# The down projection of a SwiGLU block: five contraction groups, the last by plain products, in place of four groups of Strassen products

## The chip, the cores and the metric

The kernel runs on one core of one Trainium2 chip. The metric is the device time of one execution in microseconds; 3 runs of the kernel before have a median of 3491.99 us (3489.88 to 3497.54). TensorE is called PE here, VectorE DVE, ScalarE ACT, GpSimd POOL and SyncE SP; SP issues nearly all DMAs.

## The reference, cut to what matters

One layer of a hybrid backbone for 640 tokens (512 of a latent grid, 128 of context): adaLN, attention beside a recurrent mixer, output projection, post-norm, and then the SwiGLU block, with D_MODEL = 2048 and D_FF = 5632. The change lies in the last lines of it:

```python
def _swiglu(h, p):
    return (jax.nn.silu(h @ p["w_ffn_gate"]) * (h @ p["w_ffn_up"])) @ p["w_ffn_down"]

    x = _post_norm(x, g1, _merge(att, rw, p), p["ln1_g"], p["ln1_b"])
    x = _post_norm(x, g2, _swiglu(x * (1 + sc2) + sh2, p), p["ln2_g"], p["ln2_b"])
```

`_post_norm` is a layer norm of ALPHA * x + gate * f over the 2048 features.

## The kernel before, in words

Everything is kept transposed, features on the 128 partitions and the 640 tokens along the free axis, in two halves of 320 columns (`H1`, `H2`, also called half 0 and half 1). Every fp32 matrix product is made of three fp32r matmuls, high by high, high by low and low by high, so each operand is split into a rounded part (ACT, a cast, line 1302 for the weights) and a rest (DVE, a subtraction, line 227).

The three products of the SwiGLU block go by Strassen's scheme in Winograd's form: two row tiles of the output by two column halves are made from seven products of sums of quarters instead of eight. `strassen` (from line 1451) makes one such block. It takes its weights from `Quads`, whose generator `units` loads the four quarters of a weight block (`raw`, 10 buffers), forms the three sums on POOL and DVE, splits each of the seven (`qh`, `ql`, 4 buffers each) and yields them one by one, three ahead of PE. `ORDER` (1, 7, 5, 6, 4, 2, 3) is the order of the seven products. A product of n pairs of contraction tiles is 3n matmuls of 128x128 weights by 320 columns into one PSUM bank (`b`, 8 banks).

The contraction of the down projection has 44 tiles, 22 pairs. While the gate and up projections run, `stored` writes each pair of hidden tiles to DRAM (`h_d`) as seven tiles of 128x640: splits of the quarters and of their sums. Afterwards the down projection goes in groups, `sizes = ((4, 1), (6, 2), (6, 2), (6, 2))`: pairs in the group and weight granules a round. A group is 8 rounds, j = 0 to 7, each for two row tiles of the output, so a round is 7 x 3 x 4 = 84 or 7 x 3 x 6 = 126 matmuls. The output (`z`, two tiles of 128x640 a round) starts from the normed input, and is loaded from DRAM one round ahead, added to by DVE (`gated`), and, in all groups but the last, stored to DRAM one round later (`sums_ahead`, `sums_behind`, driven by `moved` between products).

The operands of a group (tile `op`, 128x640 fp32, 7 for a pair) live in a pool of `N_F` = 63 slots that the `z` tiles share. `Fetch` loads them for the next group while one runs: one load at every second weight unit, up to `room` = 63 - 7 * pairs - 7, set in round 1 (round 3 of the first group), and in round 7 one at every unit as slots are given back. What is not loaded by then is loaded by `operand` when a product first asks for it. SP's order is the program's in this stage, so such a load stands behind what the program issued earlier, among it the store of the round before.

The last group is made in two passes, so that one half can be finished early. The first pass makes products 1, 7, 5, 6 and 3 for all rounds (90 matmuls each; half 1 is then complete and its sums for the layer norm, `norms[1].add`, go on DVE, ACT and POOL). The second pass, `rest`, makes products 2 and 4 (36 matmuls a round) in an order of PE that is fixed by hand; between its rounds PE also makes the sums of half 1 (after j = 1) and spreads mean and deviation (after j = 2), and then 16 tiles of half 1 are finished: on POOL an addition of the mean, on DVE a multiplication, on ACT scale and bias, a store. At the end half 0 is finished in the same way.

Of the kernel before, what the change touches and what calls it, by code (L numbers as in the profile page):

```python
# [8 lines left out]
F32 = mybir.dt.float32  # L9
# [6 lines left out]
P = 128  # L16
# [74 lines left out]
DONE1 = 0  # L91
NORM2 = "GTGV"
# [66 lines left out]
def step_kernel(ctx: ExitStack, tc: tile.TileContext, a: dict, o: dict, upto: int = 99, npairs: int = NPAIR, dbg=None):  # L159
# [1183 lines left out]
    class Quads:  # L1343


        def __init__(self, gen):
            self.gen = gen(self)
            self.buf, self.beside = [], None
            for _ in range(N_Q - 1):
                self.push()  # L1350
# [24 lines left out]
        def plain(self, srcs):  # L1375
            raw = []
# [7 lines left out]
        def units(self, pairs, begun=0, later=0):  # L1384


            nxt = None
            for n, src in enumerate(pairs):
                ng = src.shape[1]
                gs = range(ng)  # L1390
                whole = n < len(pairs) - later
# [27 lines left out]
                for g in gs:  # L1419
                    if whole:  # L1420
                        yield self.split(q[3, g])
                    del q[3, g]
                ahead(3)
                for g in gs:
                    if n >= begun and whole:
# [25 lines left out]
    def strassen(qs, ops, ng, out, u1=None, whole=True, beside=None):  # L1451

# [3 lines left out]
        for m in [m for m in ORDER if (m > 2 or u1 is None) and (whole or m not in (2, 4))]:  # L1456
# [4 lines left out]
            elif m == 6:  # L1461
# [5 lines left out]
                if not whole:  # L1467
                    out(0, 0, None, u1)
                    out(1, 0, None, u3)
# [104 lines left out]
    z_d = [[dram.tile([P, NT], F32, name=f"zd{c}{j}") for j in range(16)] for c in range(4)]  # L1574
# [3 lines left out]
    w_pairs += [a["w_down4"][j] for j in range(8)]  # L1578
    w_pairs += [a["w_down"][j][:, 2 * c: 2 * c + 2] for c in range(3) for j in range(8)]

    def sequence(q):
# [16 lines left out]
        yield from q.units(w_pairs, N_PRE, 8)  # L1598
        yield from q.plain(w[k, g] for w in w_pairs[-8:] for k in (1, 3) for g in range(2))
# [113 lines left out]
    def stored(i, b1, b2):  # L1713

        def put(n, x, hi, lo):
# [3 lines left out]

        p1 = fslot("p1", F32R)  # L1720
# [15 lines left out]
    class Fetch:  # L1736
# [3 lines left out]
        def __init__(self, k0, n):  # L1740
            self.k0, self.t, self.room, self.count = k0, [[None] * 7 for _ in range(n)], 0, 0
            self.every, self.turn = 2, 0
            self.order = [(i, m) for q in ((0,), (1, 2), (3, 4), (5, 6)) for i in range(n) for m in q]
# [15 lines left out]
        def operand(self, i, m):  # L1759
# [4 lines left out]
            return (t[0][:, H1], t[0][:, H2]) if q == 0 else (t[q][:, hs], t[q + 1][:, hs])  # L1764

# [52 lines left out]
    sizes = ((4, 1), (6, 2), (6, 2), (6, 2))  # L1818
# [14 lines left out]
    def moved(c, j, n):  # L1833

        rel = fetch.released(n) if fetch and j == 7 else None
        for k in range(len(ORDER)):
            if k == 4:
                sums_behind()
            if k == 3 and (c, j) != (3, 7):
# [8 lines left out]
    for c, (npr, ng) in enumerate(sizes):  # L1848
        ops, k0 = fetch, k0 + npr
        fetch = qs.beside = Fetch(k0, sizes[c + 1][0]) if c < 3 else None  # L1850
# [173 lines left out]
```

## Time and profile before

| | us |
|---|---|
| median of 3 runs (range) | 3491.99 (3489.88 to 3497.54) |
| the profiled execution | 3500.31 |
| its span, first to last instruction | 3498.5 |
| PE busy in the span | 3255.5 |
| first and last matmul of the down projection | 2857.4 and 3469.7 |

The profile is that of one execution, with times from the span's start. "Busy" is the time in which at least one instruction of the engine runs; matmuls overlap, so a mean of 309 ns for one says how long it takes, not how often one starts. A view by stages gives busy time and count (x) of each engine in a stretch, the share of its clock that TensorE was granted, the mean busy share of the 16 DMA engines and the rate. In a view of groups, "| 43.8, 647 | 7.0" is busy time in us, mean ns of one, and idle time ahead of them. A view of waits gives the total, the times and the longest.

### The profile page before, as it was taken

Reading aid. Unit: us, or ns where it says so; the run is one execution under the profiler, and the core shown is the slowest. Engines: PE = TensorE matmul, PEld = TensorE weight load, DVE = VectorE, ACT = ScalarE, POOL = GpSimd, SP = SyncE. Lnnn points to the kernel's source line nnn. Section 1 sums busy time; section 2 is a strip of 40 time slices with the busy share of each in tenths; the row PEclk is TensorE's granted clock in tenths of the full one; section 3 lists DMA queues with packets and bytes.
Section 4 is the critical chain, followed back from the end, with each engine's and each line's share of the span. In section 5 each row is a group of like instructions: output and inputs, shape, how many; then the busy total and the mean of one; then the engine's idle time right before and its main releaser. Section 6 shows DMA issues by size and latency. Waiting matters only on the chain. (4 is left out here: it accounts for less than half of the span.)

```text
span 3498.5 us, 71287 instructions
## 1 busy us (share of the span) xinstructions
PE 3255.5 (93%) x27538; PEld 2961.4 (85%) x27538; DVE 2555.3 (73%) x4562; ACT 1480.9 (42%) x3115; POOL 1070.4 (31%) x1106
## 2 busy tenths in 40 slices
PE   7988998999999689999979999999999999999987
PEld 4677676777877578899979999999999999999886
DVE  1356766776766676468688888888888888778798
ACT  1144443443443454455454444444444444334334
POOL 0021222122122132102164444444444442212245
PEclk9998999999999899999999999999999999999997
DMA  8754444444211211085434443444443478776743
GB/s 300 240 175 137 142 147 139 161 160 139 66 61 59 72 34 36 31 270 179 142 116 144 155 136 127 134 132 138 133 128 125 144 252 293 255 250 207 256 128 108
DMA packets 289717, 529.06 MB, mean 151 GB/s; under 512 B 31008, under 2 KB 83680, under 8 KB 289376
## 3 DMA queue, kind: packets, MB, share of 16 engines
q1 hardware_dynamic: 289376, 524.49, 45.3%
q8 instruction: 216, 3.54, 0.4%
q14 instruction: 125, 1.02, 0.1%
HBM read 429.65 MB, written 93.09 MB: 149 GB/s over the span
## 5 line engine op out<-in xcount | busy, mean ns | idle before, releaser
L227 DVE TENSOR_TENSOR ql<-raw,qh 128x512 fp32r<-128x512 f32 (+1 forms) x1136 | 930.6, 833 | 263.6 <-ACT qh L1302 242.5
L1302 ACT CAST qh<-raw 128x512 fp32r<-128x512 f32 (+1 forms) x1136 | 660.2, 588 | 913.2 <-PE b L113 777.8
L227 POOL TENSOR_TENSOR raw<-raw,raw 128x512 f32<-128x512 f32 (+1 forms) x288 | 394.4, 1371 | 849.6 <-DVE ql L227 662.2
L113 PE MATMUL b<-t,qh 128*128 128x320 f32 x2816 | 621.7, 310 | 8.6 <-ACT qh L1302 7.3
L113 PE MATMUL b<-op,qh 128*128 128x320 f32 x2464 | 545.9, 315 | 18.2 <-DMA op<-hd 18.0
L113 PEld LDWEIGHTS b<-t,qh 128*128 128x128 f32 x2816 | 471.5, 188 | 10.1 <-ACT qh L1302 8.1
L113 PE MATMUL b<-p,qh 128*128 128x320 f32 x2112 | 468.2, 310 | 0.0
L113 PE MATMUL b<-t,ql 128*128 128x320 f32 x1408 | 435.3, 310 | 6.4 <-DVE ql L227 6.2
L113 PEld LDWEIGHTS b<-op,qh 128*128 128x128 f32 x2464 | 417.9, 192 | 24.6 <-issue 12.3
L113 PE MATMUL b<-op,ql 128*128 128x320 f32 x1232 | 375.3, 316 | 20.1 <-DVE ql L227 20.0
L113 PEld LDWEIGHTS b<-p,qh 128*128 128x128 f32 x2112 | 355.2, 189 | 0.2 <-ACT qh L1302 0.2
L113 PE MATMUL b<-p,ql 128*128 128x320 f32 x1056 | 328.5, 311 | 8.5 <-DVE ql L227 8.5
L113 PEld LDWEIGHTS b<-t,ql 128*128 128x128 f32 x1408 | 264.4, 188 | 8.8 <-DVE ql L227 8.8
L113 PEld LDWEIGHTS b<-op,ql 128*128 128x128 f32 x1232 | 232.4, 191 | 28.5 <-DVE ql L227 28.0
L113 PE MATMUL b<-mh,qh 128*128 128x320 f32 x1024 | 231.0, 315 | 6.4 <-ACT qh L1302 6.2
L113 PE MATMUL acc<-xh,whi 128*128 128x320 f32 x928 | 233.3, 334 | 3.3 <-ACT P L1165 2.5
L113 PE MATMUL acc<-xl,whi 128*128 128x320 f32 x928 | 235.5, 336 | 0.0
L113 PE MATMUL acc<-xh,wlo 128*128 128x320 f32 x928 | 234.3, 335 | 0.0
L227 DVE TENSOR_TENSOR raw<-raw,raw 128x512 f32<-128x512 f32 (+1 forms) x288 | 217.6, 768 | 12.7 <-POOL raw L227 10.8
L113 PEld LDWEIGHTS b<-p,ql 128*128 128x128 f32 x1056 | 199.3, 189 | 11.2 <-DVE ql L227 11.2
L264 ACT CAST whi<-raw 128x512 fp32r<-128x512 f32 (+1 forms) x156 | 94.9, 608 | 232.8 <-PE acc L113 143.8
L113 PEld LDWEIGHTS b<-mh,qh 128*128 128x128 f32 x1024 | 175.4, 192 | 7.6 <-ACT qh L1302 6.8
(331 smaller groups left out, 5686.1 us busy)
## 6 DMA issues: line engine op xcount, KB each, us to landing
wm<-in_w_mod_dram SPq DMA_DIRECT2D x64, 1024.0 KB, 5.3
op<-hd SPq DMA_DIRECT2D x154, 320.0 KB, 5.7
raw<-in_w_gate_dram SPq DMA_DIRECT2D x188, 256.0 KB, 2.7
raw<-in_w_up_dram SPq DMA_DIRECT2D x188, 256.0 KB, 2.9
raw<-in_w_down_dram SPq DMA_DIRECT2D x224, 192.0 KB, 2.8
raw<-in_w_in_dram SPq DMA_DIRECT2D x132, 256.0 KB, 2.7
wm<-in_w_mod_dram SPq DMA_DIRECT2D x64, 512.0 KB, 6.2
raw<-in_w_out_dram SPq DMA_DIRECT2D x128, 256.0 KB, 3.0
```

The source lines that it names most:

```text
L113: self.eng.matmul(out, lhsT, rhs, start=start, stop=stop)
L227: eng.tensor_tensor(out=out, in0=x, in1=y, op=op)
L264: A.copy(hi, r)
L1302: A.copy(hi, x)
```

## The change

The groups become 4, 4, 4, 4 and 6 pairs. The first four go by Strassen as before, with one weight granule of 128x512 a round (the weights of 16 pairs are laid out so, not of 4). The last, six pairs, goes by eight plain products: `stored` writes four tiles for each of its pairs, not seven, and `Fetch` loads four. For rounds 0 to 3 `plain` makes both halves at once, in two banks from the same weights (144 matmuls a round); for rounds 4 to 7 half 1 alone (72), and then, in the order fixed by hand, half 0 of rounds 4 to 7, whose weights are loaded and split a second time. The sums of half 1 stand after j = 4 of that last pass, its spread and finish after j = 5. There is a fifth set of `z` tiles in DRAM.

```diff
+LAST = 6
-        def units(self, pairs, begun=0, later=0):
+        def units(self, pairs, begun, follow):
...
+                    elif follow:
+                        self.first.append(self.load(follow.pop(0)))
...
-    def strassen(qs, ops, ng, out, u1=None, whole=True, beside=None):
+    def strassen(qs, ops, ng, out, u1=None, beside=None):
...
-    def rest(qs, ops, ng, out):
-        for m, n in ((0, 2), (1, 4)):
-            out(m, 0, product(qs, ops, ng, n), None)
+    def plain(qs, ops, ng, halves, out):
+
+        npr = len(ops) // ng
+        for m in range(2):
+            ps = [bank()[:, :HN] for _ in halves]
+            for q in range(2):
+                for g in range(ng):
+                    wh, wl = qs.get()
+                    for k in range(npr):
+                        cs_ = slice(k * P, k * P + P)
+                        for t, n in zip(ps, halves):
+                            xh, xl_ = ops.plain(g * npr + k, q, n)
+                            for i, (w, x) in enumerate(((wh, xh), (wh, xl_), (wl, xh))):
+                                T.matmul(t, w[:, cs_], x, start=q + g + k + i == 0,
+                                         stop=q == 1 and i == 2 and k == npr - 1 and g == ng - 1)
+            for t, n in zip(ps, halves):
+                out(m, n, t, None)
...
-    w_pairs += [a["w_down4"][j] for j in range(8)]
-    w_pairs += [a["w_down"][j][:, 2 * c: 2 * c + 2] for c in range(3) for j in range(8)]
+    w_pairs += [a["w_down4"][j][:, c: c + 1] for c in range(4) for j in range(8)]
+    w_pairs += [a["w_down"][j] for j in range(8)]
...
-        yield from q.units(w_pairs, N_PRE, 8)
-        yield from q.plain(w[k, g] for w in w_pairs[-8:] for k in (1, 3) for g in range(2))
+
+        last = [w[k, g] for w in w_pairs[-8:] + w_pairs[-4:] for k in range(4) for g in range(2)]
+        yield from q.units(w_pairs[:-8], N_PRE, last)
+        yield from q.plain(last)
...
+        if i >= NF2 - LAST:
+            put(0, b1, fslot("p1", F32R), fslot("p1", F32R))
+            yield
+            put(2, b2, fslot("p2", F32R), fslot("p2", F32R))
+            return
...
-    sizes = ((4, 1), (6, 2), (6, 2), (6, 2))
+    sizes = (4, 1), (4, 1), (4, 1), (4, 1), (6, 2)
...
+    for j in range(8):
+        if j == 1:
+            loads.close()
+        z = ahead.pop((4, j))
+        if j == 0:
+            sums_behind()
+        if j < 7:
+            sums_ahead(4, j + 1)
+        plain(qs, ops, ng, (1, 0) if j < 4 else (1,), gated(5, 2 * j, z))
+        z1 += z
+        del z
+        summed(1, j)
+        if j < 4:
+            summed(0, j)
...
+    for j in range(4, 8):
+        plain(qs, ops, ng, (0,), gated(5, 2 * j, z1[2 * j: 2 * j + 2]))
+        for z in z1[2 * j: 2 * j + 2]:
+            norms[0].add(z)
+        if j == 4:
+            sums = norms[1].sums()
+        elif j == 5:
+            norms[1].spread(norms[1].stats(*sums, LN_EPS / ALPHA ** 2))
+            for f in range(KT):
+                finish(f, 1)
```

Up to the last pairs of the hidden layer the instructions stand on each engine as before. Three places show what moves.

SP before, in the first round of the third group (`hd105` is tile 5 of pair 10, the first pair of that group; `raw` are weights, `zd` the store of the round before):

```order
L1366 DMA raw_6806_36810<-in_w_down_dram 128x384
L1831 DMA zd214_17281<-z_6676_36272 128x640
L1831 DMA zd215_17282<-z_6677_36274 128x640
L1752 DMA op_6813_36835<-hd105_17156 128x640
L1752 DMA op_6814_36837<-hd106_17157 128x640
L1752 DMA op_6815_36842<-hd115_17163 128x640
L1752 DMA op_6816_36844<-hd116_17164 128x640
L1752 DMA op_6817_36849<-hd125_17170 128x640
L1752 DMA op_6818_36851<-hd126_17171 128x640
L1366 DMA raw_6819_36856<-in_w_down_dram 128x384
```

SP after, at the same stores, in the first round of the third group of four pairs (8 to 11; `hd116` is its last operand, `hd120` the first of the next group):

```order
L1770 DMA op_6574_35843<-hd115_17163 128x640
L1770 DMA op_6579_35866<-hd116_17164 128x640
L1367 DMA raw_6586_35905<-in_w_down4_dram 128x512
L1367 DMA raw_6590_35924<-in_w_down4_dram 128x512
L1367 DMA raw_6594_35944<-in_w_down4_dram 128x512
L1614 DMA z_6600_35971<-zd22_17269 128x640
L1614 DMA z_6601_35973<-zd23_17270 128x640
L1367 DMA raw_6603_35976<-in_w_down4_dram 128x512
L1855 DMA zd214_17281<-z_6522_35637 128x640
L1855 DMA zd215_17282<-z_6523_35639 128x640
L1770 DMA op_6619_36049<-hd120_17165 128x640
```

Before, 16 of the 42 operands of this group are issued only in its first round (six of them here), 18 in that of the second group and 16 in that of the fourth; after, 7 of the 28 operands of the second group, and none of the third, the fourth and the last.

PE before, in the last group's first pass, one product in one bank (`op_7271` and `op_7272` are high and low part of an operand):

```order
L113 MATMUL b_7555_39968<-op_7271_38795,qh_7545_39928 128x320
L113 MATMUL b_7555_39968<-op_7272_38797,qh_7545_39928 128x320
L113 MATMUL b_7555_39968<-op_7271_38795,ql_7546_39929 128x320
L113 MATMUL b_7555_39968<-op_7273_38802,qh_7545_39928 128x320
L113 MATMUL b_7555_39968<-op_7274_38804,qh_7545_39928 128x320
L113 MATMUL b_7555_39968<-op_7273_38802,ql_7546_39929 128x320
```

PE after, in the last group's rounds of both halves:

```order
L114 MATMUL b_7197_38541<-op_7081_38041,qh_7192_38515 128x320
L114 MATMUL b_7197_38541<-op_7091_38083,qh_7192_38515 128x320
L114 MATMUL b_7197_38541<-op_7081_38041,ql_7193_38516 128x320
L114 MATMUL b_7198_38542<-op_7081_38041,qh_7192_38515 128x320
L114 MATMUL b_7198_38542<-op_7091_38083,qh_7192_38515 128x320
L114 MATMUL b_7198_38542<-op_7081_38041,ql_7193_38516 128x320
```

One split of the weights (`qh`, `ql`) now serves six matmuls a tile, in two banks, where it served three.

DVE before, where the finish of half 1 begins (`ns` from `b` is the mean; `z` by `ns` the finish, `nd` and `ns` the sums of half 0, `ql` a weight's rest):

```order
L227 TENSOR_TENSOR ns_5956_33218<-b_40495,nc_33217 128x320
L227 TENSOR_TENSOR ns_5957_33219<-ns_5957_33219,nq_40481 128x320
L227 TENSOR_TENSOR z_38546<-z_38546,ns_5957_33219 128x320
L227 TENSOR_TENSOR ql_40592<-raw_40426,qh_40591 128x384
L227 TENSOR_TENSOR z_38548<-z_38548,ns_5957_33219 128x320
L236 SCALAR_TENSOR_TENSOR z_39234<-b_40573,mod,z_39234 128x320
L227 TENSOR_TENSOR z_38820<-z_38820,ns_5957_33219 128x320
L227 TENSOR_TENSOR ql_40609<-raw_40443,qh_40608 128x384
```

DVE after, at the same place:

```order
L228 TENSOR_TENSOR ns_5941_33164<-b_40315,nc_33163 128x320
L228 TENSOR_TENSOR ns_5942_33165<-ns_5942_33165,nq_40301 128x320
L228 TENSOR_TENSOR z_38460<-z_38460,ns_5942_33165 128x320
L228 TENSOR_TENSOR ql_40412<-raw_40248,qh_40411 128x384
L228 TENSOR_TENSOR z_38462<-z_38462,ns_5942_33165 128x320
L228 TENSOR_TENSOR z_38537<-z_38537,ns_5942_33165 128x320
L228 TENSOR_TENSOR ql_40427<-raw_40263,qh_40426 128x384
L228 TENSOR_TENSOR z_38539<-z_38539,ns_5942_33165 128x320
```

From this `ns` to the last `ns` of half 0 stand 64 instructions before (16 `z` by `ns`, 16 `ql`) and 42 after (16 and 12); 180 matmuls of the projection are still to come on PE before, 144 after.

More of the change, by code (lines that the diff above doesn't have):

```diff
@@ L1347, in __init__ @@
             self.gen = gen(self)
-            self.buf, self.beside = [], None
+            self.buf, self.beside, self.first = [], None, []
             for _ in range(N_Q - 1):
@@ L1375, in plain @@
         def plain(self, srcs):
-            raw = []
+            raw, self.first = self.first, []
             for src in srcs:
@@ L1449, in begin @@
         out(0, 0, product(qs, ops, ng, 2), u1)
-    def strassen(qs, ops, ng, out, u1=None, whole=True, beside=None):
+    def strassen(qs, ops, ng, out, u1=None, beside=None):
         bk = {}
-        for m in [m for m in ORDER if (m > 2 or u1 is None) and (whole or m not in (2, 4))]:
+        for m in [m for m in ORDER if m > 2 or u1 is None]:
             ps = bk[m] = product(qs, ops, ng, m)
@@ L1573, in step_kernel @@
     h_d = [[dram.tile([P, NT], F32, name=f"hd{j}{n}") for n in range(7)] for j in range(NF2)]
-    z_d = [[dram.tile([P, NT], F32, name=f"zd{c}{j}") for j in range(16)] for c in range(4)]
+    z_d = [[dram.tile([P, NT], F32, name=f"zd{c}{j}") for j in range(16)] for c in range(5)]
     w_pairs = []
@@ L1742, in __init__ @@
             self.every, self.turn = 2, 0
-            self.order = [(i, m) for q in ((0,), (1, 2), (3, 4), (5, 6)) for i in range(n) for m in q]
+            kinds = ((0, 1), (2, 3)) if k0 == NF2 - LAST else ((0,), (1, 2), (3, 4), (5, 6))
+            self.order = [(i, m) for q in kinds for i in range(n) for m in q]
         def __len__(self):
@@ L1859, in step_kernel @@
             for _ in beside:
                 pass
-            if c < 3:
-                behind += [(c, 2 * j + m, z[m]) for m in range(2)]
-            else:
-                z1 += z
+            behind += [(c, 2 * j + m, z[m]) for m in range(2)]
             del z
-            if c == 3 and j:
-                for z in z1[2 * j: 2 * j + 2] if j > 1 else z1[:4]:
-                    norms[1].add(z)
-        if c == 3:
-            order = ExitStack()
-            order.enter_context(tc.manual_schedule(engines={mybir.EngineType.PE}))
-            for j in range(8):
-                rest(qs, ops, ng, gated(5, 2 * j, z1[2 * j: 2 * j + 2]))
-                if j:
-                    for z in z1[2 * j: 2 * j + 2] if j > 1 else z1[:4]:
-                        norms[0].add(z)
-                if j == 1:
-                    sums = norms[1].sums()
-                elif j == 2:
-                    norms[1].spread(norms[1].stats(*sums, LN_EPS / ALPHA ** 2))
-                    for f in range(KT):
-                        finish(f, 1)
-            order.close()
@@ L1884, in step_kernel, with summed @@
-        del ops
+        del ops
+    def summed(n, j):
+        if j:
+            for z in z1[2 * j - 2 * (j == 1): 2 * j + 2]:
+                norms[n].add(z)
+    for j in range(8):
[12 more added lines that the diff above has]
+            summed(0, j)
@@ new lines, in step_kernel @@
+    order = ExitStack()
+    order.enter_context(tc.manual_schedule(engines={mybir.EngineType.PE}))
+    for j in range(4, 8):
[8 more added lines that the diff above has]
+                finish(f, 1)
+    order.close()
```

32 lines of the change are left out of this document (16 added, 16 removed).

## The prediction

> **What bounds the kernel now.** The page comes first.
>
> ```profile
> span 3498.5 us, 71287 instructions
> PE 3255.5 (93%) x27538; PEld 2961.4 (85%) x27538; DVE 2555.3 (73%) x4562; ACT 1480.9 (42%) x3115; POOL 1070.4 (31%) x1106
> ```
>
> PE is busy for 93% of the span, so time lies in its work or in its few waits. The profiled execution took 3500.31 us around this span; the median of the runs is 3491.99, 0.2% less. Next the view of one tile, `op`, which every matmul of the down projection reads.
>
> ```profile
> L113 PE MATMUL b<-op,qh x2464: 302/309/636, 2857.4 to 3469.6; 128*128 128x320 f32 x190
> L113 PE MATMUL b<-op,ql x1232: 303/309/637, 2857.7 to 3469.7; 128*128 128x320 f32 x176
> ```
>
> All 3696 are there (22 pairs x 7 products x 8 rounds x 3), so counting them off in order dates every round (rounds are counted from 0). The view of stages below is cut at such rounds. A row starts with the stretch and its length, then PE, PEld, DVE, ACT and POOL busy, the clock, the DMA share and GB/s.
>
> ```profile
> 2700.00:2800.00 100.00, 100.00 (x684) 100.00 (x683) 82.82 (x112) 43.88 (x77) 44.03 (x33) 1.00 0.41 132
> 2857.38:2908.82 51.44, 50.41 (x338) 49.32 (x337) 46.00 (x86) 26.26 (x44) 15.96 (x12) 1.00 0.89 323
> 2908.82:2958.11 49.29, 49.29 (x339) 49.29 (x337) 43.97 (x87) 21.93 (x38) 13.18 (x9) 1.00 0.83 293
> 2958.11:2988.50 30.39, 23.62 (x129) 20.25 (x128) 17.73 (x39) 7.22 (x15) 4.17 (x4) 0.89 0.86 315
> 2988.50:3117.86 129.36, 129.36 (x885) 129.36 (x884) 107.19 (x214) 52.52 (x105) 31.14 (x28) 1.00 0.65 219
> 3117.86:3145.16 27.30, 21.93 (x129) 20.41 (x128) 16.85 (x35) 7.31 (x15) 3.97 (x4) 0.87 0.91 326
> 3274.51:3298.45 23.94, 17.79 (x92) 16.02 (x91) 16.99 (x32) 5.47 (x11) 7.76 (x6) 0.79 0.88 310
> 3298.45:3409.48 111.03, 99.29 (x633) 94.21 (x633) 101.44 (x191) 43.30 (x92) 47.64 (x37) 0.98 0.48 156
> 3414.76:3430.05 15.29, 15.09 (x116) 14.30 (x115) 15.29 (x33) 7.11 (x16) 8.68 (x7) 1.00 0.43 121
> 3430.05:3469.71 39.66, 32.44 (x180) 30.59 (x180) 38.69 (x62) 21.33 (x43) 27.40 (x25) 0.83 0.34 111
> 3469.71:3498.50 28.79, 17.96 (x59) 10.58 (x57) 19.69 (x33) 11.10 (x20) 12.90 (x13) 0.55 0.26 92
> ```
>
> The second group's rounds 1 to 7 are 882 matmuls in 129.36 us: 146.7 ns each, PE without a gap. Rounds 4 to 7 of the first group (336 in 49.29) keep the same pace. Against it the other stretches lose: start of group one 51.44 - 49.28 = 2.2; first round of groups two, three and four 11.9, 8.8 and 10.7 (126, 126 and 90 matmuls); the rest of group four's first pass, 630 matmuls, 18.6; rounds 1-2 of its second pass, 72 matmuls, 4.7; rounds 3-7, 180 matmuls, 13.3. That is 70 us of stall. The view of waits, from 2840 us on, names the two causes:
>
> ```profile
> PE b L113 <- DVE ql L227: 20.0, 25, 1.7
> PE b L113 <- DMA op<-hd: 18.0, 12, 5.0
> ```
>
> The first round of a group waits for operands from DRAM; in group four DVE is busy for 101.44 of 111.03 us, then 15.29 of 15.29 and 38.69 of 39.66, and sets the pace.
>
> **The change, part by part.** *Matmuls.* Sixteen pairs by seven products are 2688 matmuls, six by eight 1152: 3840, 144 more, +21.1 us at 146.7 ns. Plain products read weights and operands in another order, but this trace has such a stage, the output projection (tile `mh`):
>
> ```profile
> L113 PE MATMUL b<-mh,qh x1024: 302/309/634, 1490.0 to 1733.4; 128*128 128x320 f32 x171
> 1700.00:1720.00 20.00, 20.00 (x138) 20.00 (x137) 12.24 (x22) 8.26 (x15) 2.65 (x3) 1.00 0.51 151
> ```
>
> The median is the same 309 ns and about 137 fit into 20 us, so I price both kinds alike: 2688 x 0.1467 = 394.2 us and 1152 x 0.1467 = 169.0.
>
> *Group boundaries.* SP's timeline at the first boundary, and three rows of the view of DMA issues (2857 to 3470 us):
>
> ```profile
> 2952.44 1.66 SPq L1752 DMA_DIRECT2D op<-hd  x2
> 2960.77 2.13 SPq L1366 DMA_DIRECT2D raw<-in_w_down_dram  x2
> 2963.24 1.42 SPq L1752 DMA_DIRECT2D op<-hd  x3
> ...
> 2980.16 5.52 SPq L1752 DMA_DIRECT2D op<-hd  x8
> op<-hd SPq DMA_DIRECT2D x134, 320.0 KB, 5.7
> z<-zd SPq DMA_DIRECT2D x61, 320.0 KB, 5.2
> raw<-in_w_down_dram SPq DMA_DIRECT2D x25, 256.0 KB, 5.3
> ```
>
> By SP's order 18, 16 and 16 operand loads come only in a group's first round, because 63 slots less 42 and 7 leave room for 14; at the first boundary SP stood from 2954.1 to 2960.77 besides, and three more (2963.24) came late, 21. With four pairs the room is 28, the whole next group. After the change 7 loads are late at the first boundary (fetching starts in round 3 there), none at the other three. Two costs: in proportion (53 loads, 31.4 us) 7 cost 4.1; a line through the counts (21 at 11.9, 16 at 9.75 on the mean) has 2.9 us fixed and gives 5.9. From below: 320 KB at 315 GB/s are 1.0 us, so seven arrive some 9 us after the boundary with 2 us of waiting behind the z store, and product six needs them after 60 matmuls, 8.8 us; the stall may be near nothing. I take 4.0 (0 to 5.9), and 0.5 (0 to 2.9) at each of the other three, 1.5.
>
> *Rounds of four pairs.* Such a round moves 3.5 operands, four z transfers (320 KB each) and four weight tiles of 256 KB: 3.5 MB in 12.32 us, 285 GB/s. Group one's rounds 4 to 7 already moved 293 GB/s with DVE at 43.97 of 49.29, and lost nothing. The fifth pass over z is in these figures. SP's queue has 11.5 issues to make, at most 0.69 us each (the 8 loads in 5.52), so 7.9 us of 12.32. I take 0 per round, and the start loss of 2.2 stays.
>
> *Last group.* Its combinations of weights on POOL and DVE go. DVE's own rows, 3298 to 3409 us:
>
> ```profile
> L227 DVE TENSOR_TENSOR ql<-raw,qh 128x384 fp32r<-128x384 f32 x69 | 43.8, 647 | 7.0 <-ACT qh L1302 7.0
> L227 DVE TENSOR_TENSOR ns<-ns,nq 128x320 f32<-128x320 f32 x13 | 9.9, 765 | 0.0
> L227 DVE TENSOR_TENSOR nd<-z,nc 128x320 f32<-128x320 f32 x13 | 7.1, 545 | 0.0
> L236 DVE SCALAR_TENSOR_TENSOR z<-c,mod,z 128x192 f32<-128x192 f32 x13 | 6.8, 526 | 0.0
> L236 DVE SCALAR_TENSOR_TENSOR z<-c,mod,z 128x128 f32<-128x128 f32 x13 | 5.8, 449 | 0.0
> ```
>
> A round of one half has 8 splits and two each of the others: 5.18 + 1.53 + 1.09 + 1.05 + 0.90 = 9.75 us beside 72 matmuls, 10.56. A round of both halves has 21.1 us for about 14. So DVE ceases to set the pace, narrowly. Four both-half rounds (0 to 3) and four of half 1 (4 to 7): 864 x 0.1467 = 126.7, and 2.0 for the narrowness (0 to 4). Rounds 4 and 5 of half 0: 21.1, and the 4.7 of today's rounds 1-2, where PE also does the sums and the spread.
>
> *Last two rounds and the tail.* Here the finish of half 1 falls on DVE and POOL. Today, 3433.2 to 3450.3 us, and the two ends of that stage:
>
> ```profile
> L227 POOL TENSOR_TENSOR z<-z,ns 128x320 f32<-128x320 f32 x16 | 17.3, 1118 | 0.0
> L227 DVE TENSOR_TENSOR z<-z,ns 128x320 f32<-128x320 f32 x7 | 7.6, 1088 | 0.8 <-POOL z L227 0.8
> L227 DVE TENSOR_TENSOR ql<-raw,qh 128x384 fp32r<-128x384 f32 x5 | 6.1, 1216 | 0.0
> L227 DVE TENSOR_TENSOR nd<-z,nc 128x320 f32<-128x320 f32 x2 | 2.3, 1156 | 0.0
> L227 DVE TENSOR_TENSOR ns<-ns,nq 128x320 f32<-128x320 f32 x2 | 1.5, 734 | 0.2 <-ACT nq L239 0.2
> 3432.08 0.48 DVE L227 TENSOR_TENSOR ns<-b,nc 128x320 f32<-128x320 f32 x1
> 3474.73 2.29 PE L113 MATMUL b<-one,ns 128*64 128x1 f32 x20 [4.70 <-POOL ns L227]
> ```
>
> From DVE's mean (3432.08) to the last sums (3474.73) 64 DVE instructions take 42.65 us, 0.67 each. After the change 42 stand there: 28.0. But beside POOL's 16, DVE did just 16 instructions with two SBUF inputs in 17.3 us; of the 37 such in the new stage 21 remain, at about 0.5 (the 0.48 of the row above is one alone), two more with one such input (1.0), and four POOL adds, each holding DVE up by some 0.6 (1156 ns for `nd` beside POOL, 545 elsewhere), 2.4: together 31.2. I take 29.5, and 2.0 ahead of it (3430.05 to 3432.08). If PE set the stage it were 21.1 + 5.0 - 2.0 = 24.1. The Trainium skill, page SBUF — State Buffer, "Who interferes with whom", says that a VectorE instruction with two SBUF inputs and a GpSimd one that reads SBUF exclude each other. The 16 beside 16 agree; by that rule alone the sum would be 1.7 us higher. By the mean alone it is 1.5 lower. The rest, 3474.73 to 3498.5, keeps its 23.8.
>
> *At nothing:* 18 fewer stores of hidden operands, with their casts, lie under a stage where PE runs 100.00 of 100.00 us (2700 to 2800, DVE 82.82).
>
> *Sum* from 2857.4: 394.2 + 2.2 + 4.0 + 1.5 + 126.7 + 2.0 + 21.1 + 4.7 + 2.0 + 29.5 + 23.8 = 611.7, against 641.1 today: 29.4 us less, a span of 3469.1. Off the median: 3462.6, say 3463.
>
> **Rivals.** *A boundary has a fixed price.* The line's 2.9 us, or more where SP waits for the z store, falls due four times, 5.9 + 3 x 2.9 in place of 5.5, and DVE stays tight at 4 for 2 and 31.2 for 29.5: 12.8 worse, 3475. For it: SP's stand at the first boundary. Against: it stood before a weight load of a group whose weights come in two granules a round and, with their sums, fill all ten `raw` buffers; a four-pair round has one granule and takes five.
>
> *DVE never binds at the end and boundaries vanish:* 5.5 + 2.0 + 5.4 = 12.9 better, 3450. Against: 38.69 busy of 39.66.
>
> *Slower: the DMA engines do not hold 285 GB/s* through three more groups. The change breaks even where 24 rounds lose 29.4 us: 12.32 + 1.22 = 13.54 us a round, 259 GB/s; below that it is slower. At 240 GB/s a round takes 14.6, 24 x 2.3 = 55 us more: 3518. For it: the six-pair rounds were shown at 219 only. Against: 293 sustained over four rounds, 326 at a share of 0.91.
>
> *Slower: only PE's work counts*, and the 70 us of stall come back under other names: 3491.99 + 21.1 = 3513. The Trainium skill, page Perfetto Trace Analysis, "Identifying the Most-Contended Engine", says to optimize the most occupied engine first; this change loads it. Against: the stall is larger than the addition.
>
> **How the numbers follow.** Forecast 0.68, fixed price 0.14, no bind 0.10, DMA 0.05, PE's work 0.03. The range, 3449 to 3480, takes in the first three, with the terms' bounds and some 4 us of the median's own spread. A measurement of this kernel can tell about 0.2%, 7 us, from no change. The first three cases lie further below than that: 0.92, of which I move 0.03 to "same" for bounds that add up badly.
>
> **What would show it.** Right: four-pair rounds at 12.32 us in all four groups; PE's wait for `op` under 5 us in total; last-group rounds at 21.1 and 10.6 us with DVE under 95%; 55 us from the start of the last two rounds to the end, where today 3430.05 to 3498.5 are 68.4. Wrong: rounds over 13.5 us at a DMA share above 0.9, or PE waits for weights or z where `op` stood.

## The result, and the profile after

| | before | after |
|---|---|---|
| median of 4 runs each (range), us | 3494.76 (3489.88 to 3501.88) | 3467.11 (3459.87 to 3469.55) |
| the profiled execution, us | 3500.31 | 3459.87 |
| down projection in it, first `op` matmul to the end, us | 641.1 | 609.9 |

The ratio of the times is 0.9918, with a 95% interval of 0.9903 to 0.9933: 27.7 us faster, where 29.4 were forecast. The two profiled executions lie 40.4 us apart; 31.2 us of that are the down projection, and 9.1 lie ahead of it, where the order of the instructions is the same up to the last pairs of the hidden layer. In the profiles of this study the first `op` matmul starts anywhere from 2848.2 to 2866.4 us, whatever was changed behind it. So from here on kernels are compared by the down projection alone, from that matmul to the end of the span. Each of these is one execution, and the first group, the same in ten of the kernels, loses 3.3 to 4.9 us in nine of them and 0.5 in one; so where down projections differ by little, the rows by stage decide.

The page after the change, and the view of the tile `op`:

```profile
span 3458.1 us, 70966 instructions
PE 3254.0 (94%) x27682; PEld 2972.3 (86%) x27682; DVE 2499.6 (72%) x4478; ACT 1449.3 (42%) x3031; POOL 999.1 (29%) x1034
L114 PE MATMUL b<-op,qh x2560: 302/309/555, 2848.2 to 3432.3; 128*128 128x320 f32 x197
L114 PE MATMUL b<-op,ql x1280: 303/309/635, 2848.5 to 3432.4; 128*128 128x320 f32 x183
```

The share of PE hardly tells that anything happened: 144 matmuls more and PE busy 1.5 us less. The view of stages does. Its rows are the first group's first round and a later one, the second group's first two rounds, groups three and four whole, the both-half rounds, the rounds of half 1, rounds 4 and 5 of half 0, its last two rounds up to the sums, and the rest:

```profile
2848.24:2860.58 12.34, 12.34 (x86) 12.31 (x85) 9.03 (x15) 6.83 (x11) 3.51 (x3) 1.00 1.04 396
2873.27:2886.62 13.35, 13.01 (x86) 12.33 (x85) 10.67 (x21) 5.95 (x10) 2.55 (x2) 1.00 1.02 361
2950.50:2964.33 13.83, 12.99 (x87) 12.38 (x86) 12.54 (x25) 3.65 (x7) 4.11 (x2) 1.00 0.72 253
2964.33:2977.91 13.58, 12.59 (x87) 12.32 (x86) 10.85 (x19) 4.89 (x9) 3.16 (x2) 1.00 0.81 298
3052.57:3249.69 197.12, 197.12 (x1347) 197.12 (x1345) 179.95 (x353) 68.44 (x128) 46.47 (x31) 1.00 0.78 276
3249.69:3335.24 85.55, 85.55 (x582) 85.23 (x581) 43.70 (x85) 22.61 (x47) 14.59 (x11) 1.00 0.46 148
3335.24:3377.48 42.24, 42.24 (x290) 42.24 (x289) 36.24 (x69) 20.09 (x42) 9.76 (x10) 1.00 0.50 144
3377.48:3402.51 25.03, 25.03 (x186) 24.56 (x184) 18.70 (x38) 10.80 (x22) 5.56 (x6) 1.00 0.51 144
3402.51:3434.92 32.41, 26.32 (x145) 24.64 (x144) 29.06 (x41) 17.20 (x33) 23.99 (x21) 0.84 0.29 99
3434.92:3458.10 23.18, 13.21 (x56) 10.02 (x56) 14.86 (x26) 9.69 (x17) 9.81 (x9) 0.59 0.32 113
```

Groups three and four are 1344 matmuls in 197.12 us, 146.7 ns each, and PE is busy all of it, boundaries included. The waits of PE from 2840 us on, which were 20.0 us for `ql` and 18.0 for `op` before, are now:

```profile
PE b L114 <- DVE ql L228: 5.3, 6, 1.7
PE b L114 <- POOL ns L228: 2.2, 1, 2.2
PE b L114 <- ACT qh L1303: 1.1, 2, 0.8
PE b L114 <- DMA op<-hd: 0.7, 1, 0.7
```

Term by term, in us, with a loss being the length of a stretch less its matmuls at 146.7 ns:

| term of the forecast | forecast | measured |
|---|---|---|
| 2688 Strassen matmuls, rounds of four pairs at 12.32 | 394.2 | 394.2 |
| loss in the first group | 2.2 | 3.7 |
| loss at the first boundary and in the group behind it | 4.0 | 3.5 |
| the other three boundaries | 1.5 | 0.0 |
| both-half rounds and rounds of half 1 (126.7 + 2.0) | 128.7 | 127.8 |
| rounds 4 and 5 of half 0 (21.1 + 4.7) | 25.8 | 25.0 |
| last two rounds to the sums (2.0 + 29.5) | 31.5 | 32.4 |
| the rest | 23.8 | 23.2 |
| sum | 611.7 | 609.9 |

### The profile page after: what moved, and what is told of

The parts are those of the page before. It is cut to its first block, busy times and chain, and to the rows that moved or that the text cites. A ratio compares the mean times of both kernels' runs of the same rounds, so it can differ in the third digit from the quotient of the medians.

```text
span 3458.1 us, 70966 instructions
## 1 busy us (share of the span) xinstructions
PE 3254.0 (94%) x27682; PEld 2972.3 (86%) x27682; DVE 2499.6 (72%) x4478; ACT 1449.3 (42%) x3031; POOL 999.1 (29%) x1034
## 4 chain that ended last, share of the span: by engine, by line
PE 58%; DVE 6%; ACT 2%; issue 2%; DMA 1%; POOL 1%; SPq 0%; ACTq 0%; DVEq 0%; POOLq 0%
PE b L114 50%; PE acc L114 4%; PE m L114 2%; DVE z L228 1%; DVE ql L228 1%; POOL z L228 1%; PE x L114 1%; ACT z L240 0%; PE acc L118 0%; DVE smx L1165 0%; DVE pr L228 0%; ACT P L1166 0%; DVE ip L228 0%; DVE raw L228 0%; DMA raw<-in_w_down_dram 0%
## 5 line engine op out<-in xcount | busy, mean ns | idle before, releaser
L228 DVE TENSOR_TENSOR ql<-raw,qh 128x512 fp32r<-128x512 f32 (+1 forms) x1064 | 887.8, 849 | 260.4 <-ACT qh L1303 247.1
L1303 ACT CAST qh<-raw 128x512 fp32r<-128x512 f32 (+1 forms) x1064 | 633.3, 610 | 830.6 <-PE b L114 647.2
L228 POOL TENSOR_TENSOR raw<-raw,raw 128x512 f32<-128x512 f32 x240 | 354.4, 1477 | 804.4 <-DVE ql L228 546.2
L114 PE MATMUL b<-op,qh 128*128 128x320 f32 x2560 | 553.2, 311 | 1.9 <-ACT qh L1303 1.1
L114 PEld LDWEIGHTS b<-op,qh 128*128 128x128 f32 x2560 | 425.9, 189 | 4.4 <-ACT qh L1303 2.7
L228 DVE TENSOR_TENSOR raw<-raw,raw 128x512 f32<-128x512 f32 x240 | 185.4, 780 | 12.5 <-POOL raw L228 9.4
```

Source lines behind the costliest of these rows:

```text
L114: self.eng.matmul(out, lhsT, rhs, start=start, stop=stop)
L228: eng.tensor_tensor(out=out, in0=x, in1=y, op=op)
L1303: A.copy(hi, x)
```

## The experiments

The theory after this: late operand loads make the stall at a boundary, in proportion to their number; the grouping and the plain last group gain about half each; DMA has room; and in the last two rounds DVE, beside POOL, sets the pace. The main rivals: a fixed price for a boundary, DMA near its edge, and for the last stage another cause (the order in which DVE's work is queued, a cover too short). All kernels below start from the changed one, unless it is said otherwise.

**Late loads: more of them.** The room for early loads is cut from group to group.

```diff
-                fetch.room = N_F - 7 * npr - 7
+                fetch.room = (28, 14, 7, 0)[c]
```

> Only the number of operands that may be loaded ahead is cut: room 14, 7 and 0 in the second, third and fourth group instead of 28, so that by SP's order 8 loads are late at the third group's first round, 15 at the fourth's and some 17 of 24 at the last group's (7 at the second's, as in the changed kernel). Theory, the stall of a boundary is that of its late loads, about 0.6 us each once they outlast what hides them: 3 to 5 us for 8, 8 to 10 us for 15, 8 to 12 us for 17, where the changed kernel has 0.0 at all three. Rival, a boundary has a fixed price or none, whatever is loaded late: all three stay within 1 us of the changed kernel.

Down projection 627.2 us, 17.3 more. By SP's order 7, 8, 15 and 17 loads come late at the four boundaries. The first rounds behind them:

```profile
2952.39:2965.77 13.38, 12.93 (x86) 12.37 (x85) 12.44 (x25) 3.65 (x7) 4.07 (x2) 1.00 0.65 228
3053.82:3067.71 13.89, 13.09 (x86) 12.33 (x85) 12.54 (x25) 3.89 (x8) 3.30 (x2) 1.00 0.74 264
3156.45:3173.19 16.74, 14.09 (x86) 13.85 (x85) 13.10 (x26) 4.37 (x8) 2.66 (x2) 0.90 1.04 400
3259.94:3290.43 30.49, 24.29 (x147) 23.76 (x146) 7.00 (x15) 4.10 (x8) 0.00 (x0) 0.89 0.90 326
```

The groups behind them lose 2.9, 4.1, 4.9 and 9.4 us (the last is its first round alone, against 21.12 in the changed kernel). A boundary has no fixed price: the three that cost nothing in the changed kernel cost something as soon as loads are late. The losses go by when SP issues a load. Of the 15 at the third of these boundaries seven went out from 3152.74 us on, ahead of the group's first matmul (3156.45), and only eight behind it and behind the store of the round before:

```profile
3162.38 5.14 SPq L1770 DMA_DIRECT2D op<-hd  x8
```

Counted by what SP issues behind the group's first matmul, 7, 8, 8 and 18 loads are late, at 0.41, 0.51, 0.61 and 0.52 us each; in the kernel before it is 21, 16 and 16 at 0.57, 0.55 and 0.67. The third boundary's 4.9 us miss the 8 to 10 that were expected of 15 late loads; the other two are in their ranges. In the last two rows of the view by stages the DMA share is 1.04 and 0.90 and the clock is 0.90 and 0.89.

**Late loads: none.** The first group fetches from round 1 on, as the others do.

```diff
-            if j == (1 if c else 3):
+            if j == 1:
```

> The first group starts to load the next group's operands in round 1 and not in round 3, so that none of the 28 is late at the first boundary. Theory, the late loads are that boundary's stall: the second group's first round goes from 13.83 to 12.32 us, its second, 13.58, comes down too, 1.5 to 3.5 us in all. Rival, DMA is full in the first group's first rounds (share 1.02 to 1.04 in rounds 0 and 2): the 3.7 us that these rounds lose grow by as much, and nothing is gained.

Down projection 605.3 us, 4.6 less. The first boundary's round now takes 12.32 us. The whole group behind it:

```profile
2952.38:3051.19 98.81, 98.81 (x674) 98.57 (x673) 89.70 (x177) 34.26 (x64) 25.27 (x16) 1.00 0.80 282
```

The 3.5 us of the second group are gone (0.25 left), and the first group's own loss fell too, from 3.7 to 2.0, though it now carries more loads. Loading earlier cost the first group nothing (2.0 to 3.1 us in the three kernels that do it).

**The last stage without POOL.** Half 1's finish adds the mean on DVE, not on POOL.

```diff
-NORM3 = "G"
+NORM3 = "V"
```

> The finish of half 1 adds the mean on DVE and not on POOL: 16 POOL instructions fewer and 16 DVE instructions more in the last two rounds. Theory, POOL and DVE alternate there one for one, so POOL's 16 cost DVE more than they save it: the stage from DVE's mean to the last sums falls from 33.3 to 27 to 29 us, PE setting it (21.1 and some 5 of lag). Rival, DVE's time goes by its count (33.3 us for 42, 0.79 each): 58 instructions take 46 us, 12 us longer.

From DVE's mean to the last sums 33.5 us, against 33.3 in the changed kernel (3401.59 to 3434.92): neither expectation came. In the changed kernel POOL's sixteen additions and DVE's work beside them read so (POOL's timeline, then DVE's groups from 3402.6 to 3420 us):

```profile
3402.63 17.44 POOL L228 TENSOR_TENSOR z<-z,ns 128x320 f32<-128x320 f32 x16
```

```profile
L228 DVE TENSOR_TENSOR z<-z,ns 128x320 f32<-128x320 f32 x9 | 9.7, 1108 | 0.8 <-POOL z L228 0.8
L228 DVE TENSOR_TENSOR ql<-raw,qh 128x384 fp32r<-128x384 f32 x5 | 6.1, 1224 | 0.0
L228 DVE TENSOR_TENSOR nd<-z,nc 128x320 f32<-128x320 f32 x1 | 1.1, 1146 | 0.0
L228 DVE TENSOR_TENSOR ns<-ns,nq 128x320 f32<-128x320 f32 x1 | 0.8, 817 | 0.1
```

Again 16 with two SBUF inputs beside POOL's 16. With POOL out of it, DVE's timeline has 28 steps of 0.40 us in one block, and behind the block stands the split for which PE waits (second fence, PE):

```profile
3406.14 11.33 DVE L228 TENSOR_TENSOR z<-z,ns 128x320 f32<-128x320 f32 x28
3417.39 1.48 DVE L228 TENSOR_TENSOR ql<-raw,qh 128x384 fp32r<-128x384 f32 x3
```

```profile
3417.99 0.64 PE L114 MATMUL b<-op,ql 128*128 128x320 f32 x1 [7.25 <-DVE ql L228]
```

So the single step got faster by 0.7 us, and the stage not at all. In the changed kernel DVE made only 5 splits during POOL's 17.4 us, in which PE at its pace of 9 matmuls a split could use 13; here one long block ahead of the splits does as much harm.

**A longer cover.** Half 1's sums go into the middle of round 4 and their spread behind it, so that the finish lies beside three rounds in place of two.

```diff
-        plain(qs, ops, ng, (0,), gated(5, 2 * j, z1[2 * j: 2 * j + 2]))
+        plain(qs, ops, ng, (0,), gated(5, 2 * j, z1[2 * j: 2 * j + 2]),
+              (lambda: got.append(norms[1].sums())) if j == 4 else None)
...
-        if j == 4:
-            sums = norms[1].sums()
-        elif j == 5:
-            norms[1].spread(norms[1].stats(*sums, LN_EPS / ALPHA ** 2))
+        if j == 4:
+            norms[1].spread(norms[1].stats(*got[0], LN_EPS / ALPHA ** 2))
```

> Sums and spread of half 1 stand one round earlier in PE's order (the sums in the middle of round 4, the spread after it), so that the finish has three rounds of matmuls beside it and not two. Theory, the last stage is set by DVE and POOL and needs more cover: from the start of round 4 of half 0 to the last sums 57.4 us now, 52 to 54 then. Rival, PE comes to wait for the sums of half 1 and the spread in the earlier place, or DVE's work is in the way wherever it stands: 57 us or more.

Down projection 610.9 us; the half-0 rounds with the sums take 57.5 us (3383.97 to 3441.50) against 57.4. The four rounds lose 12.74 us against 12.71: the loss had only moved from rounds 6 and 7 to rounds 5 and 6. No gain.

**The grouping alone.** Groups of 4, 4, 4, 4 and 6, the last by Strassen in two passes; made from the kernel before.

```diff
-    sizes = ((4, 1), (6, 2), (6, 2), (6, 2))
+    sizes = (4, 1), (4, 1), (4, 1), (4, 1), (6, 2)
```

> Groups of 4, 4, 4, 4 and 6, the last by Strassen in two passes as before the change, so only the grouping is left of the change (3696 matmuls again). About 17 of the last group's loads come late. Theory (grouping and plain products are worth about half of the gain each): 394.2 + 3.7 + 3.5 for the groups of four, then the 224.0 us that the kernel before took from its last group's first matmul to the end: down projection about 626 us (621 to 632), 15 less than before, 16 more than the changed kernel. Rival (the grouping alone brings nothing, the stall comes back in the one boundary that is left): 636 or more. Rival (the plain last group brings nothing): 615 or less.

**The plain last group alone**, behind groups of 4, 6 and 6:

```diff
-    sizes = (4, 1), (4, 1), (4, 1), (4, 1), (6, 2)
+    sizes = ((4, 1), (6, 2), (6, 2), (6, 2))
```

> Groups of 4, 6, 6 and 6 as before the change, the last by plain products, so only the plain last group is left of the change. Theory: the first three groups keep the 417.1 us of the kernel before, stalls of 11.9 and 8.8 us at their boundaries included; the last keeps the 208.4 us of the changed kernel, and some 10 of its 24 loads, late now, add 3 to 6: down projection about 630 us (626 to 634), 11 less than before. Rival (the two parts only pay together, since 144 more matmuls cost 21 us and DVE stays tight): 638 or more.

Down projections of 620.3 and 626.6 us: alone the grouping brings 20.8 us, the plain last group 14.5, together 31.2. Of the 4.1 between, 2.1 lie from the last group on: its first round loses 10.7 us before, 8.8 with the grouping alone and nothing with plain products, so what the grouping saves there can't be saved twice. The other 1.9 lie ahead of it, mostly in the first group, which lost 0.5 us in one kernel and 3.7 in the other. In the kernel with the grouping alone, groups three and four, the last group's first round, and what follows it in its first pass:

```profile
3067.69:3264.81 197.12, 197.12 (x1347) 197.12 (x1345) 179.81 (x352) 68.29 (x128) 47.44 (x33) 1.00 0.81 283
3264.81:3286.81 22.00, 16.28 (x93) 15.15 (x92) 17.26 (x34) 5.46 (x11) 7.07 (x6) 0.84 0.76 256
3286.81:3396.52 109.71, 98.42 (x634) 94.34 (x633) 103.79 (x190) 43.00 (x92) 43.70 (x36) 0.98 0.49 160
```

With the plain last group alone, the first rounds of groups two and three, and the last group's:

```profile
2957.06:2987.40 30.34, 24.43 (x128) 21.77 (x127) 17.61 (x39) 7.32 (x15) 4.54 (x4) 0.83 0.86 320
3116.76:3143.53 26.77, 22.09 (x128) 20.85 (x127) 17.01 (x36) 7.41 (x15) 3.98 (x4) 0.87 0.91 327
3272.89:3294.01 21.12, 21.12 (x146) 21.12 (x145) 6.73 (x15) 4.11 (x8) 0.00 (x0) 1.00 0.67 220
```

Each half of the change removes its own stalls and leaves the other's where they were. Both expectations were 3 to 6 us too high, the first just outside its range. The first kernel's first group lost 0.5 us, not 3.7, and its last boundary 8.8, not 10.7. In the second no load of the last group was late (24 operands where Strassen needs 42; SP issued the last at 3267.75 us, 5 us ahead), where ten were expected.

**DMA's margin.** One, two and four useless copies a round in groups two, three and four:

```diff
+            if k == 1:
+                for _ in range(load[c]):
+                    DMA.dma_start(out=junk.pop(), in_=h_d[0][0])
```

> The changed kernel with 1, 2 and 4 copies of 320 KB from DRAM to DRAM more in every round of the second, third and fourth group; nothing reads them. Rounds of 3.5 MB become 3.8, 4.1 and 4.8 MB: 311, 338 and 391 GB/s, if a round stays at 12.32 us. Theory (at 285 GB/s the DMA engines have room, by the 326 at a share of 0.91 seen before the change): 12.3 to 12.5 us a round with one copy and with two, slower only with four, 13 us or more. Rival (285 is at the edge already): each copy adds its whole 1.1 us, 13.4, 14.5 and 16.8 us a round.

The three groups, and the first four rounds and a bit of the last of them:

```profile
2959.65:3060.25 100.60, 99.56 (x674) 98.62 (x673) 91.06 (x175) 34.77 (x64) 28.28 (x16) 1.00 0.89 326
3060.25:3159.23 98.98, 98.98 (x675) 98.56 (x673) 90.89 (x175) 34.17 (x64) 25.77 (x16) 1.00 0.91 335
3159.23:3262.42 103.19, 99.94 (x674) 98.56 (x673) 88.47 (x182) 35.48 (x64) 19.25 (x15) 1.00 0.94 362
3159.23:3210.00 50.77, 50.41 (x344) 50.02 (x343) 45.65 (x95) 17.18 (x31) 10.27 (x8) 1.00 1.00 379
```

With one copy the group loses 2.0 us (the changed kernel 3.5), with two 0.4, with four 4.6; four rounds then ran at 12.3 to 12.4 us, 379 GB/s and a share of 1.00, before the rounds grew to 13 and 14 us. With two copies 335 GB/s, some 17% above 285, cost next to nothing. The rival is out.

**The last stage without the finish.** Half 1's normalisation is left out: 32 instructions of DVE and POOL are not done, and half 1 of the output is not normed.

```diff
-        norms[n].apply(z, (NORM2, NORM3)[n][f % len((NORM2, NORM3)[n])])
+        if n == 0:
+            norms[n].apply(z, NORM2[f % len(NORM2)])
```

> The changed kernel without the normalisation in half 1's finish (32 instructions of DVE and POOL left out; its affine step on ACT and its stores stay). Theory (the finish, queued on DVE between the splits of the weights that PE needs next, makes the last stage's loss): the four half-0 rounds lose 4 to 5.5 us in place of 12.7, sums and spread alone, and the span falls by about 8 us to 3450. Rival (PE waits there for something else: loads of weights, banks, its own sums): 10 us or more of the loss stay, span 3456 or more.

Down projection 600.9 us, 9.0 less, and the four rounds lose 3.87 us in place of 12.71: this is what the sums and the spread cost, and the finish costs the other 8.8. (The span is 3457.6, not 3450, since the first `op` matmul came 8.5 us later.) Half 0's rounds and sums without the finish, and in the changed kernel:

```profile
3386.90:3435.56 48.66, 46.42 (x331) 45.69 (x329) 32.67 (x62) 19.56 (x40) 9.21 (x10) 1.00 0.32 92
```

```profile
3377.48:3434.92 57.44, 51.35 (x330) 49.20 (x328) 47.77 (x78) 28.00 (x55) 29.55 (x26) 0.91 0.39 119
```

The matmuls are the same, but PE is busy with them 4.9 us longer (51.35 - 46.42) at a clock of 0.91. Waits for splits are 3.9 us. The two make the 8.8 us.

**DVE's order by hand.** That the finish sits ahead of splits suggested that its place in DVE's queue is what costs. So DVE's order is written out from round 4 on, with the earlier spread, both steps on DVE, and one finish behind two of every three weight granules of rounds 5 to 7:

```diff
-    order.enter_context(tc.manual_schedule(engines={mybir.EngineType.PE}))
+    order.enter_context(tc.manual_schedule(engines={mybir.EngineType.PE, mybir.EngineType.DVE}))
...
                     for k in range(npr):
...
+                    if beside:
+                        next(beside, None)
```

> The changed kernel with half 1's sums in the middle of round 4 of the last pass and their spread after it, as in the experiment one round earlier, and with DVE's order written out in that pass: one whole finish, both steps on DVE, behind two of every three weight splits of rounds 5, 6 and 7. DVE's work is the same or more. Theory (what costs is the place of the finishes in DVE's queue, ahead of splits, and POOL's steps beside them): 24 splits, 16 finishes and 6 tiles' other steps are about 0.48 x 24 + 0.81 x 16 + 1.3 x 6 = 32.3 us beside 31.7 us of matmuls, so the four half-0 rounds lose 4 to 6 us in place of 12.7, and the down projection takes 601 to 604 us in place of 609.9. Rival (DVE's work as a sum is too much for these rounds, wherever it stands): 10 us or more of the loss stay, down projection 607 or more.

Down projection 616.6 us, worse by 6.7. PE's waits from 3379 to 3443 us:

```profile
PE b L114 <- DVE m L234: 4.2, 1, 4.2
PE b L114 <- POOL ns L228: 3.8, 1, 3.8
PE b L114 <- DVE ql L228: 2.9, 2, 2.0
```

A written order has its own traps: the statistics (`m`) stood on DVE behind round 4's last sums, and PE waited 4.2 us for them; a square on ACT between two of DVE's steps held up a split for 2.0.

**The same with the earlier fetch**, in five rounds against the kernel before:

> The changed kernel with the fetch for the second group from round 1 on and one finish per granule, both as in the experiments of those names. Theory (the two are independent): down projection 597 to 600 us, 605.3 less what the other gains; against the kernel before a ratio of 0.987 to 0.990. Rival (one eats the other up): no better than the changed kernel's 0.992.

3468.16 us against 3495.05, ratio 0.9925 (0.9910 to 0.9940); down projection 612.8. No better than the changed kernel: the earlier fetch gave its 4 us (nothing lost at the first boundary) and the order took them.

**The order mended.** The statistics stand right behind the sums, each round's last steps go among the next round's splits, and no finish stands in the last four granules:

```diff
+    def placed():
+        fs = iter(range(KT))
+        for i in range(24):
+            late = norms[0].late(todo.pop(0)) if todo else None
+            if late:
+                next(late)
+            if i % 6 != 5 and i < 20 or late:
...
+                    finish(f, 1)
+            if late:
+                next(late, None)
+            yield
```

> As one finish per granule, but without the two waits in DVE's written order that cost there 4.2 us (statistics behind round 4's last sums) and 2.0 us (a square on ACT between two of DVE's steps): the statistics stand straight behind the sums, each round's last two steps go among the next round's splits, and no finish stands among the last four granules of round 7. Theory (place in the queue): the four half-0 rounds lose 5 to 8 us in place of 12.7, down projection 602 to 606 us in place of 609.9. Rival (DVE's work as a sum): 10 us or more of loss, 608 or more.

Down projection 609.1 us, 0.8 less than the changed kernel; the four rounds lose 10.78 us. Round 5 ran with five finishes at 10.66 us, without loss, but rounds 6 and 7 took 12.68 and 15.21. From the spread to DVE's last split:

```profile
3393.70:3429.40 35.70, 31.70 (x206) 30.24 (x206) 35.05 (x71) 22.64 (x43) 6.05 (x6) 0.98 0.43 136
```

DVE is busy for 35.05 of 35.70 us. It starts with a lead of three granules, has used it up by round 6, and PE then waits for it. The loss of 5 to 8 us that the place theory asks for did not come, and DVE's work as a sum binds in this order. That it would bind in any order is not shown, because the sum depends on the order. These are the 32 steps of the finish here, and below them in the kernel with the finish on DVE, from its mean on:

```profile
L228 DVE TENSOR_TENSOR z<-z,ns 128x320 f32<-128x320 f32 x32 | 18.9, 591 | 0.6
```

```profile
L228 DVE TENSOR_TENSOR z<-z,ns 128x320 f32<-128x320 f32 x32 | 13.5, 491 | 0.0
```

They take 5.4 us more here. The second step on a tile starts some 0.52 us behind the first, where steps in the block start every 0.40, and six of the sixteen second steps take about 1 us, each beside one of POOL's additions for the sums of half 0. Less those 5.4 us DVE's 35.05 would be 29.7, about what PE's 206 matmuls in this stretch need (30.2). An order that keeps the two steps on a tile apart, and both away from POOL's additions, was not run.

**The mended order with the earlier fetch**, in five rounds:

> The kernel of the run before this one, with the fetch for the second group from round 1 on. Theory (the two gains are independent): down projection 597 to 602 us, and a ratio to the kernel before of 0.987 to 0.990. Rival (the gains overlap or the order of DVE does not hold): 605 or more, a ratio no better than 0.991.

3459.52 us against 3492.07, ratio 0.9902 (0.9886 to 0.9919); down projection 603.5, both between the two expectations. It is the fastest of the kernels timed in rounds, but its interval overlaps the changed kernel's, so that it beats it is not shown; 4.6 of the 6.4 us between the two down projections are what the earlier fetch brings alone.

The last stage of all of these, in us: loss of half 0's four rounds; less the 3.87 without finish; PE's waits for DVE in them; PE busy (rounds and sums) above the 46.42 without finish; mean clock.

| kernel | loss | less 3.87 | waits | busy above 46.42 | clock |
|---|---|---|---|---|---|
| changed kernel | 12.71 | 8.8 | 3.9 | 4.9 | 0.91 |
| finish on DVE | 12.83 | 9.0 | 7.3 | 1.7 | 0.94 |
| one round earlier | 12.74 | 8.9 | 6.2 | 2.7 | 0.97 |
| one finish per granule | 16.40 | 12.5 | 7.1 | 5.4 | 0.91 |
| one finish per granule, earlier fetch | 17.11 | 13.2 | 7.1 | 6.1 | 0.88 |
| order mended | 10.78 | 6.9 | 3.9 | 2.9 | 0.97 |
| order mended, earlier fetch | 9.24 | 5.4 | 3.9 | 1.4 | 1.00 |

In each row waits and added busy time make up the loss to within 0.2 us, as they should, since PE either waits or is busy. The last two kernels have the same instructions there and the same four waits, and differ by 1.5 us, all of it in PE's busy time.

## Why the prediction was right, point by point

*The 70 us of stall.* That waits, not PE's work, could be bought back with 144 matmuls was the main claim, and it held: PE's waits for `op` fell from 18.0 to 0.7 us, for `ql` from 20.0 to 5.3. But the two rows that were to name the causes of the 70 us hold 38 of them. From the first to the last `op` matmul PE stood for 38.5 us before (612.33 less 573.84 busy) and for 7.3 after (584.20 less 576.90), and the matmuls lost 70.1 and 20.9; the rest of the loss is PE at work more slowly, at a clock of 0.97 and 0.99 on the mean. The forecast priced whole stretches, so it had this share in its numbers, though not in its account.

*Boundaries.* That late loads make the stall is shown, by taking loads away (605.3) and by making them late (627.2); in proportion holds roughly, at 0.41 to 0.67 us a load over three kernels. The first one's 4.0 was right (3.5). PE's waits there are 0.7 us for an operand and 1.0 for a split of weights, which the prediction had named as a sign of being wrong; without the late loads the two rounds lose nothing. The other three, priced at 0.5 each for want of a reason for nothing, cost nothing. The line with 2.9 us fixed, and with it the rival of a fixed price, is out.

*Rounds of four pairs at 12.32.* Right in groups three and four to the last matmul, not in all four as the prediction's sign had it. The first group lost 3.7 us, not the 2.2 of today; that it lost 0.5 in the kernel with the grouping alone and 2.0 to 4.9 in the others says that this term differs between kernels in which the group is the same. PE's waits in it are for splits of weights (1.1 and 0.3 us in the changed kernel), and no run here settles why.

*DMA.* The break-even at 259 GB/s was never near. The three groups needed 276 to 298, and 379 were held for four rounds.

*Both-half and half-1 rounds.* DVE ceased to set the pace: 43.70 of 85.55 us busy and 36.24 of 42.24. Of the 2.0 us set aside for narrowness 1.1 was used.

*Last two rounds and tail.* The size was right (32.4 against 31.5, and 55.6 against 55 to the end), but as a sum of two misses that cancel: from DVE's mean to the sums it took 33.3 us where 29.5 were forecast, and the mean came 0.9 us ahead of the stage (3401.59, stage from 3402.51) where 2.0 us behind was forecast. The step priced the stage as DVE's instructions in a row. What the runs show in its place: DVE runs without a pause only up to its last split at 3429.5 us, then PE makes what is left and DVE waits for it; and the 3.9 us that PE waits on the way cost it 4.9 more at a lower clock. The rule of the page SBUF — State Buffer ("Who interferes with whom") in the Trainium skill, that such pairs exclude each other, agrees with 16 beside 16 at 1.1 us, and by it the sum would have been 31.2, nearer to the 33.3. But with POOL's additions on DVE the stage stayed as long, since they then stood in one block ahead of a split: the exclusion is one way in which the finish holds up the splits, and not the only one.

*At nothing:* the smaller hidden stores cost nothing. From the output projection's first matmul to the first `op` matmul it is 1367.4 us before (1490.0 to 2857.4) and as much after within 0.1.

*The rivals.* A fixed price is refuted above. "DVE never binds at the end" is half true: the boundaries vanish but for one, the end does bind. "Only PE's work counts" is refuted: PE got 3.9% more matmuls in this stage (144 on 3696) and the stage got 31.2 us shorter. The Trainium skill, page Perfetto Trace Analysis, "Identifying the Most-Contended Engine", says to optimize the most occupied engine first. That engine was PE, at 93%, and the gain did come from its waits; so this case does not speak against the rule, only against reading it as a ban on giving that engine more work.

## What to carry to other kernels

A stall is priced by what comes late, not by the boundary at which it shows: count the loads that the queue issues behind the boundary, at the buffers' real room, and give each its share. More work on the busiest engine can pay where it takes work from the engine that holds it up; look for rows where the busiest engine waits and another is busy nearly all the time (91 to 100% here). Before work is moved about beside a stage, add up what the other engine must do up to the last thing that is waited for, with times from a trace of that very order, since the same 32 steps took 13.5 us in one order and 18.9 in another. Here an earlier start and another engine for one step brought nothing, the orders that were tried a little at best, and only leaving the finish out brought the whole 8.8 us.

## What the runs showed of the hardware

*Short waits of PE can halve its clock.* The changes of the granted clock (the column behind POOL's) lie, in each of the 14 traces, on one grid of steps of 3.41 us. The changed kernel's last stage, cut at such changes:

```profile
3411.75:3415.16 3.41, 1.70 (x10) 1.44 (x11) 3.41 (x5) 1.61 (x3) 3.41 (x4) 1.00 0.31 110
3415.17:3425.40 10.23, 8.69 (x31) 7.89 (x32) 10.23 (x16) 6.50 (x13) 5.98 (x6) 0.50 0.27 96
3425.41:3428.82 3.41, 3.41 (x25) 3.41 (x25) 3.41 (x9) 3.25 (x7) 3.30 (x1) 1.00 0.49 169
```

PE's timeline has its four waits there:

```profile
3412.80 0.42 PE L114 MATMUL b<-op,ql 128*128 128x320 f32 x1 [1.73 <-DVE ql L228]
3415.04 0.54 PE L114 MATMUL b<-op,ql 128*128 128x320 f32 x1 [0.65 <-DVE ql L228]
3418.33 0.63 PE L114 MATMUL b<-op,ql 128*128 128x320 f32 x1 [0.61 <-DVE ql L228]
3422.02 0.64 PE L114 MATMUL b<-op,ql 128*128 128x320 f32 x1 [0.92 <-DVE ql L228]
```

In the step before the drop PE stood for 1.71 us (3.41 less 1.70), in parts of the first two waits; then the clock is 0.50 for three steps, 31 matmuls in 8.69 us of busy time. In the last two kernels of the table the same waits came with the drop in one profile and without it in the other. With the order mended they left a step with 1.59 us of standing (3.41 less 1.82), and the drop followed:

```profile
3424.86:3428.27 3.41, 1.82 (x10) 1.56 (x11) 3.38 (x7) 1.30 (x3) 1.00 (x1) 1.00 0.13 48
3428.27:3431.68 3.41, 3.41 (x14) 3.41 (x14) 1.11 (x3) 0.00 (x0) 0.00 (x0) 0.50 0.16 53
```

With the earlier fetch they fell otherwise on the grid, no step of the four rounds had more than 1.47 us, and the clock stayed at 1.00 there. Counted over all 14 traces, from 2840 us to 25 us before the end: of the steps at full clock, all 26 in which PE stood for 1.75 us or more were followed by 0.50, 3 of the 12 between 1.35 and 1.75, and none below. What a wait costs thus depends on where it falls, which no kernel here controls. The Trainium skill, page TensorE: Matmul & The Clock Gate, "What's actually happening", puts the half clock behind an idle window of about 3.4 us that runs freely; the 0.50 and the steps of 3.41 us agree, but here a step that PE stood through by half was enough, and no wait ahead of the drop was longer than 1.73 us.

*DMA went beyond what was assumed.* The first group's first round moved 396 GB/s at a share of 1.04, and lost nothing.
